# A weighted running average over 16 sequences: all v loads plain and rounded by VectorE, stores issued two slots later, the first state step moved

## The chip, the cores and the metric

The kernel runs on one core of a Trainium2 chip. The metric is the time of one execution on the device in microseconds (us). The median of four runs of the kernel before is 293.57 us (293.37 to 294.54).

The engines go by the names of the profile: PE is TensorE (matmul), PEld its weight loads, DVE is VectorE, ACT is ScalarE, POOL is GpSimd, and SP is SyncE, which here only issues DMAs. Each engine takes its instructions strictly in the order of the program; an instruction that waits holds up all behind it on that engine.

## The reference

For each of 16 batches and 256 channels a recurrence runs over 2048 time steps. Inputs are w and u (256 numbers each) and k and v (16 x 2048 x 256, float32, 33.55 MB each); the output has v's shape. Cut to what is computed:

```
for b, t:
    ww = u + k[b,t];  qq = max(pp, ww)
    e1 = exp(pp - qq);  e2 = exp(ww - qq)
    output[b,t] = (e1*aa + e2*v[b,t]) / (e1*bb + e2 + 1e-08)
    ww = pp - w + k[b,t];  qq = max(ww, k[b,t])
    e1 = exp(ww - qq);  e2 = exp(k[b,t] - qq)
    aa = e1*aa + e2*v[b,t];  bb = e1*bb + e2;  pp = qq
```

So every output is a quotient of two running sums, a numerator that carries v and a denominator without it, with a running maximum pp taken out of the exponents. Every input is read once (67.1 MB) and every output written once (33.5 MB).

## The kernel before, in words

**Tiles and slots.** Time is cut into 16 steps of 128 (NST), and the batches into 4 groups of 4. One tile n (64 of them, NP) is 128 time steps of 4 batches, 128 partitions by 1024 numbers, 512 KB of k and 512 KB of v. Tile n belongs to step c = n // 4. One turn of the main loop is a slot. Slots 0 to 9 (L427 to L447) only start tiles; from slot 10 on (L448 to L483), slot n starts tile n and also finishes the denominator of tile q = n - 10 (LAG is 10) and the numerator and output of tile qp = n - 11. After the last tile a closing loop (L487 to L510) finishes the remaining ones.

**What one tile needs.** `load_k` and `load_v` bring it in. `round_k` (L182, DVE) rounds k to float32r in `km`. `logs` (L191, L197, PE) makes exponents in PSUM out of k and of the decays. `exps` (L208 in the first ten slots, L210 later, ACT) turns them into weights in the ring EZR, which holds 12 tiles. `cast_v` (L223, DVE) rounds v to bf16 in `vb`. `times_v` (L228, DVE) multiplies the weights with vb, in EZR too. `sums` (L252, PE) adds up each half step for the state. Ten slots later `den` (L358, PE) makes the denominators, `recip` (L364 and L366, ACT: a logarithm and an exponential) their reciprocals in a buffer `rd`, `num` (L371, PE) the numerators, half a tile at a time in one PSUM bank NUMB, and `mult` (L375, DVE) the output, in place in rd. `store` (L378) sends rd out.

**Two kinds of v load.** `v_mode` says "dma" for n >= 10 with n % 4 == 3 (14 tiles): there GpSimd issues a DMA that converts float32 to bf16 on the way, straight into vb (L68), and `cast_v` does nothing. The other 50 v loads are plain loads by SyncE (L71), rounded by DVE.

**SyncE's queue.** At the head of slot n SyncE is given the loads six tiles ahead (AHEAD), for n + 6 < 16 as v of tile n + 5 and k of tile n + 6, later as k and v of tile n + 6; near the end of slot n the store of tile n - 11. The buffers are 6 for k, 5 for v, 4 for vb, 6 for rd; an issue waits until the buffer's last user is done. GpSimd issues the converting load of tile 4c + 11 in `state_next` of step c.

**The state.** Each step c needs one pass of small work that takes its sums to the ring: `copy_sums`, `turn`, `state_logs` (L274, ACT), `state_frames` (L283), `state_scan` (L287, DVE), `state_offsets` (L296 to L300), `state_weights` (L304, ACT), `state_chain` (L313 to L318, DVE), `turn_back` (L337, PE), `inject` (a cast on DVE, L343, and four DMAs of 8 KB by GpSimd into EZR, L348), `state_next` (L327, L328, GpSimd). Frames and offsets are on DVE for steps 0, 1 and 15, on GpSimd for the others. The list `plan` (L391 to L407) names for each of them a slot, counted from s = 4c + 3, and a place within the slot; `small_work(n, place)` issues what is due there. Step 0's state is first needed by the denominators of tile 0 to 3 in slots 10 to 13.

Of the kernel before, what the change touches and what calls it, by code (L numbers as in the profile page):

```python
# [7 lines left out]
F32 = mybir.dt.float32  # L8
F32R = mybir.dt.float32r
BF16 = mybir.dt.bfloat16  # L10
ALU = mybir.AluOpType
ACT = mybir.ActivationFunctionType
# [3 lines left out]
def kernel(  # L16
# [9 lines left out]
    K = tc.keep_in_program_order  # L26
    PE, DVE, SC, POOL, SP = nc.tensor, nc.vector, nc.scalar, nc.gpsimd, nc.sync

    B, T, Dm = k.shape
# [4 lines left out]
    NP = 4 * NST  # L34
    RING = 12
    AHEAD = 6
    LAG = 10
# [5 lines left out]
    kpool = ctx.enter_context(tc.tile_pool(name="kpool", bufs=AHEAD))  # L43
    vpool = ctx.enter_context(tc.tile_pool(name="vpool", bufs=5))
    vbpool = ctx.enter_context(tc.tile_pool(name="vbpool", bufs=4))
    rpool = ctx.enter_context(tc.tile_pool(name="rpool", bufs=6))
    small = ctx.enter_context(tc.tile_pool(name="small", bufs=2))
    tiny = ctx.enter_context(tc.tile_pool(name="tiny", bufs=1))
    ps = ctx.enter_context(tc.tile_pool(name="ps", bufs=1, space=bass.MemoryType.PSUM))


    kr_of, vr_of, VB = {}, {}, {}

    def v_mode(n):
        return "dma" if n >= LAG and n % 4 == 3 else "dve"

    def rows_of(x, n):
        c, p = divmod(n, 4)
        return x[4 * p:4 * p + 4, c * TC:(c + 1) * TC, :].rearrange("n t d -> t n d")

    def load_k(n, queue=SP):
        kr_of[n] = kpool.tile([128, 4, Dm], F32, tag="kr", name="kr")
        K(queue.dma_start(out=kr_of[n], in_=rows_of(k, n)))

    def load_v(n, queue=SP):
        if v_mode(n) == "dma":
            VB[n] = vbpool.tile([128, 4, Dm], BF16, tag="vb", name="vb")
            K(POOL.dma_start(out=VB[n], in_=rows_of(v, n)))  # L68
        else:
            vr_of[n] = vpool.tile([128, 4, Dm], F32, tag="vr", name="vr")  # L70
            K(queue.dma_start(out=vr_of[n], in_=rows_of(v, n)))  # L71


    def load(n):
        for x, f in ((n - 1, load_v), (n, load_k)) if n < LAG + AHEAD else ((n, load_k), (n, load_v)):
            if x < NP and (f == load_k or v_mode(x) != "dma"):
                f(x)

# [32 lines left out]
    load_k(1)  # L113
    load_row(SP, 1, 2, u)
    load_v(0)
    for n in range(2, AHEAD):
        load_k(n)
# [62 lines left out]
    def round_k(n):  # L180
        km = consts.tile([128, 4, Dm], F32R, tag=f"km{n % 2}", name="km") if n < 2 else KM[n - 2]
        K(DVE.tensor_copy(km, kr_of.pop(n)))  # L182
        KM[n] = km
# [21 lines left out]
    def exps(n):  # L205
        if n < TURNS:
            for q in range(2):
                K(SC.activation(ez(n)[:, q], half(n, q), ACT.Exp))  # L208
        else:
            K(SC.activation(ez(n)[:, 0:2], PS[:, 0:4, :].rearrange("p (q i) x -> p q i x", q=2), ACT.Exp))  # L210

    def cast_v(n):
        mode = v_mode(n)
        if mode == "dma":
            return
        vb = vbpool.tile([128, 4, Dm], BF16, tag="vb", name="vb")
        vr = vr_of.pop(n)
        if mode == "act":
            K(SC.activation(vb, vr, ACT.Copy))
        elif mode == "pool":  # L220
            K(POOL.tensor_copy(vb, vr))
        else:
            K(DVE.tensor_copy(vb, vr))  # L223
        VB[n] = vb

    def times_v(n):
        vb = VB.pop(n).rearrange("p (i n) d -> p i (n d)", i=2)
        K(DVE.tensor_mul(ez(n)[:, 2:4], ez(n)[:, 0:2], vb.unsqueeze(1).broadcast_to([128, 2, 2, D])))  # L228
# [94 lines left out]
    def state_next(c):  # L323
        G, tb = st.pop((c, "G")), st.pop((c, "tb"))
        AB, nxt = AB_of[c % 2], AB_of[(c + 1) % 2]
        y = tiny.tile([128, 2, 32], F32, tag="y", name="y")
        K(POOL.tensor_mul(y, AB[:, :, 1, :], G[:, 1, :].unsqueeze(1).broadcast_to([128, 2, 32])))  # L327
        K(POOL.tensor_add(nxt[:, :, 0, :], y, tb[:, :, 1, :]))  # L328

        if 4 * c + 11 < NP:  # L330
            load_v(4 * c + 11)


    def turn_back(c):
        t = MISC[:, Dm:Dm + 128]
# [19 lines left out]
    def den(n):  # L355
        for m, q in (("L", 0), ("Id", 1)):
            for i in range(2):
                K(PE.matmul(DENB[:, i, :], mats[m], ez(n)[:, q, i, :], start=q == 0, stop=q == 1,  # L358
                            skip_group_check=True))
# [9 lines left out]
    def num(n, bank, i):  # L369
        for m, q in (("LN", 2), ("IdN", 3)):  # L370
            K(PE.matmul(bank, mats[m], ez(n)[:, q, i, :], start=q == 2, stop=q == 3, skip_group_check=True))  # L371

    def mult(n, bank, i):
        rd = RD[n]
        K(DVE.tensor_mul(rd[:, i, :], bank, rd[:, i, :]))  # L375

    def store(n):
        K(SP.dma_start(out=rows_of(out, n), in_=RD.pop(n).rearrange("p i (n d) -> p (i n) d", n=2)))  # L378
# [10 lines left out]
    for c in range(NST):  # L389
        s = 4 * c + 3  # L390
        plan = [(s + 1, "act" if s + 1 < LAG else "recip", copy_sums), (s + 1, "pe", turn),  # L391
                (s + 2, "act", state_logs), (s + 2, "mid", state_frames), (s + 2, "scan", state_scan), (s + 2, "scan", state_offsets),
                (s + 3, "recip", state_weights), (s + 3, "chain", state_chain),
                (s + 4, "nums", turn_back), (s + 4, "mid", inject), (s + 4, "mid", state_next)]
        if c == 0:
            plan = [(s + 1, "act", copy_sums), (s + 1, "pe", turn), (s + 2, "act", state_logs),
                    (s + 2, "chain", state_frames), (s + 2, "chain", state_scan), (s + 2, "chain", state_offsets),
                    (s + 3, "act", state_weights), (s + 3, "chain", state_chain),
                    (s + 4, "logs", turn_back), (s + 4, "logs", inject), (s + 4, "round", state_next)]
        if c == 1:  # L400
            plan = [(s + 1, "act", copy_sums), (s + 1, "pe", turn), (s + 2, "act", state_logs),
                    (s + 2, "chain", state_frames), (s + 2, "chain", state_scan), (s + 2, "chain", state_offsets)] + plan[6:]
        if c == NST - 1:
            plan = [(s + 1, "copy", copy_sums), (s + 1, "turn", turn),
                    (s + 1, "post", state_logs), (s + 1, "mid", state_frames), (s + 1, "mid", state_scan), (s + 1, "mid", state_offsets),
                    (s + 2, "post", state_weights), (s + 2, "first", state_chain),
                    (s + 3, "turn", turn_back), (s + 3, "first", inject)]  # L407
        for slot, where, f in plan:
            later.setdefault((slot, where), []).append((f, c))

    def small_work(n, where):
        for f, c in later.pop((n, where), []):
            f(c)
# [10 lines left out]
    logs(0)  # L424
    round_k(1)
    cast_v(0)
    for n in range(LAG):  # L427

# [19 lines left out]
    for n in range(LAG, NP):  # L448

        q, qp = n - LAG, n - LAG - 1  # L450
        load(n + AHEAD)
        if qp >= 0:
            num(qp, NUMB, 0)
        den(q)
        small_work(n, "nums")
        exps(n)
        small_work(n, "act")
        if qp >= 0:
            mult(qp, NUMB, 0)
        small_work(n, "mid")  # L460
        if n + 2 < NP:
            round_k(n + 2)
        if n + 1 < NP:
            cast_v(n + 1)
        else:
            times_v(n)
        if qp >= 0:
            num(qp, NUMB, 1)

        sums(n - 1)  # L470
        recip(q, lambda: small_work(n, "recip"))
        if qp >= 0:
            mult(qp, NUMB, 1)
        small_work(n, "scan")
        if qp >= 0:
            store(qp)
        if n + 1 < NP:
            times_v(n)
            small_work(n, "chain")
            logs(n + 1)  # L480
        else:
            den(q + 1)
        small_work(n, "pe")  # L483
    sums(NP - 1)
    small_work(NP, "copy")
    late = []
    for n in range(NP, NP + LAG + 1):  # L487

        q, qp = n - LAG, n - LAG - 1
        H = PS[:, 2 * (n % 2):2 * (n % 2) + 2, :]  # L490
        for i in range(2):
            num(qp, H[:, i, :], i)
        small_work(n, "turn")
        if q < NP:
            recip(q, lambda: small_work(n, "recip"))
        small_work(n, "post")
        if q + 1 < NP:
            den(q + 1)
        small_work(n, "first")
        if qp == NP - 1:  # L500
            last_outputs(qp, H)
            break
        late.append((qp, H))
        if n != NP + 1:

            for x, bank in late:
                mult(x, bank, slice(0, 2))
                store(x)
            late = []
        small_work(n, "mid")  # L510
# [31 lines left out]
```

## Time and profile before

| what | value |
|---|---|
| median of the runs | 293.57 us (293.37 to 294.54, 4 runs) |
| the profiled execution's own time | 294.03 us |
| its span, first to last instruction | 292.3 us |
| busy: PE, DVE, ACT, POOL | 262.7, 256.2, 257.0, 119.4 us |
| granted clock of TensorE | 0.996 of full speed |
| HBM read and written | 67.12 MB and 33.55 MB, 344 GB/s over the span |
| SyncE's queue; GpSimd's queue | 93.08 MB; 4.20 MB |
| k load, v load, store, converting load: issue to landing | 9.1, 9.1, 8.6, 8.7 us |
| DVE: one L375, L182, L223, L228 | 732, 716, 720, 1216 ns |
| ACT: one L210, L364, L366 | 1875, 1013, 1046 ns |
| DVE waiting for a k tile | 12.9 us, 28 times |

A profile comes from one execution. Busy time is that in which an engine has an instruction in work; issuing DMAs and waiting are not counted. A row of groups reads: line, engine, operation, what it writes and reads, how often, then busy time and the mean of one in ns, then how long the engine stood idle just before them and what it was waiting for. The slices are 40 equal parts of the span (7.3 us each), with the busy share in tenths. GB/s counts a transfer by the bytes that it writes, so a converting load counts half of what it reads.

### The profile page before, as it was taken

Reading aid. Unit: us, or ns where it says so; the run is one execution under the profiler, and the core shown is the slowest. Engines: PE = TensorE matmul, PEld = TensorE weight load, DVE = VectorE, ACT = ScalarE, POOL = GpSimd, SP = SyncE. Lnnn points to the kernel's source line nnn. Section 1 sums busy time; section 2 is a strip of 40 time slices with the busy share of each in tenths; the row PEclk is TensorE's granted clock in tenths of the full one; section 3 lists DMA queues with packets and bytes.
Section 4 is the critical chain, followed back from the end, with each engine's and each line's share of the span. In section 5 each row is a group of like instructions: output and inputs, shape, how many; then the busy total and the mean of one; then the engine's idle time right before and its main releaser. Section 6 shows DMA issues by size and latency. Waiting matters only on the chain. (4 is left out here: it accounts for less than half of the span.)

```text
span 292.3 us, 4969 instructions
## 1 busy us (share of the span) xinstructions
PE 262.7 (90%) x1694; PEld 119.8 (41%) x1694; DVE 256.2 (88%) x439; ACT 257.0 (88%) x253; POOL 119.4 (41%) x226
## 2 busy tenths in 40 slices
PE   6997898999999999998898999998899989988881
PEld 1443433445444444443443444444344444433330
DVE  4699999999999999998989999897998989886753
ACT  2586788999999999999899999989899998999892
POOL 7000425453535445554534455551455545242200
PEclk9999999999999999999999999999999999999998
DMA  6999999999999999999999999999999999974686
GB/s 222 349 348 348 348 306 347 300 386 315 382 340 372 362 350 381 333 379 332 379 344 372 375 336 383 330 380 330 376 372 337 380 335 383 329 276 152 217 290 215
DMA packets 103522, 97.86 MB, mean 335 GB/s; under 512 B 4157, under 2 KB 103497, under 8 KB 103497
## 3 DMA queue, kind: packets, MB, share of 16 engines
q1 hardware_dynamic: 93752, 93.08, 94.5%
q0 software_dynamic: 9440, 4.20, 10.0%
q8 instruction: 13, 0.21, 0.3%
q10 hardware_dynamic: 304, 0.27, 0.3%
q14 instruction: 13, 0.10, 0.1%
HBM read 67.12 MB, written 33.55 MB: 344 GB/s over the span
## 5 line engine op out<-in xcount | busy, mean ns | idle before, releaser
L210 ACT ACTIVATE EZR<-PS 128x2048 bf16<-128x2048 f32 x54 | 101.3, 1875 | 6.3 <-PE PS L197 5.4
L375 DVE TENSOR_TENSOR rd<-PS,rd 128x512 f32<-128x512 f32 (+1 forms) x118 | 86.1, 732 | 7.7 <-PE PS L371 6.6
L228 DVE TENSOR_TENSOR EZR<-EZR,vb 128x2048 bf16<-128x2048 bf16 x64 | 77.8, 1216 | 3.5 <-ACT EZR L208 2.6
L366 ACT ACTIVATE rd<-rd 128x1024 f32<-128x1024 f32 (+1 forms) x65 | 68.0, 1046 | 1.2
L364 ACT ACTIVATE rd<-PS 128x1024 f32<-128x1024 f32 (+1 forms) x65 | 65.9, 1013 | 2.0 <-PE PS L358 1.8
L348 POOL DMA_DIRECT2D EZR<-cb x64 | 38.5, 607 | 61.4 <-DVE cb L343 49.6
L371 PE MATMUL PS<-EZR,LN 128*128 128x512 bf16 x128 | 48.6, 380 | 11.9 <-DVE rd L375 8.1
L182 DVE CAST km<-kr 128x1024 fp32r<-128x1024 f32 x64 | 45.8, 716 | 13.1 <-DMA kr<-in_k_dram 12.9
L197 PE MATMUL PS<-km,NLE 128*128 128x512 f32 x128 | 47.6, 454 | 2.3 <-DVE km L182 2.0
L371 PE MATMUL PS<-EZR,IdN 128*128 128x512 bf16 x128 | 48.4, 378 | 0.0
L197 PE MATMUL PS<-km,NLZ 128*128 128x512 f32 x128 | 41.0, 402 | 0.0
L358 PE MATMUL PS<-EZR,L 128*128 128x512 bf16 x128 | 38.0, 379 | 1.8 <-ACT rd L364 1.7
L358 PE MATMUL PS<-EZR,Id 128*128 128x512 bf16 x128 | 38.1, 379 | 0.0
L223 DVE CAST vb<-vr 128x1024 bf16<-128x1024 f32 x50 | 36.0, 720 | 0.0
L191 PE MATMUL PS<-WU,CO 32*128 32x512 bf16 x256 | 26.4, 391 | 2.3 <-DVE WU L423 1.9
L283 POOL TENSOR_TENSOR F<-LL,LL 128x32 f32<-128x32 f32 x13 | 7.6, 583 | 51.0 <-ACT LL L274 51.0
L208 ACT ACTIVATE EZR<-PS 128x1024 bf16<-128x1024 f32 x20 | 19.4, 1021 | 8.7 <-PE PS L197 8.7
L197 PEld LDWEIGHTS PS<-km,NLZ 128*128 128x128 f32 x128 | 24.6, 192 | 5.8
L197 PEld LDWEIGHTS PS<-km,NLE 128*128 128x128 f32 x128 | 19.4, 191 | 17.5 <-issue 12.7
L252 PE MATMUL PS<-EZR,OH 128*32 128x256 bf16 x512 | 25.8, 278 | 0.1
L371 PEld LDWEIGHTS <-IdN 128*128 128x128 bf16 x128 | 12.4, 97 | 27.7 <-issue 24.9
L296 POOL TENSOR_TENSOR Q<-P,F 128x64 f32<-128x64 f32 x13 | 15.6, 1203 | 13.0 <-DVE P L287 13.0
(72 smaller groups left out, 212.5 us busy)
## 6 DMA issues: line engine op xcount, KB each, us to landing
kr<-in_k_dram SPq DMA_DIRECT2D x64, 512.0 KB, 9.1
out_dram<-rd SPq DMA_DIRECT2D x63, 512.0 KB, 8.6
vr<-in_v_dram SPq DMA_DIRECT2D x50, 512.0 KB, 9.1
vb<-in_v_dram POOLq DMA_DIRECT2D x14, 256.0 KB, 8.7
EZR<-cb POOLq DMA_DIRECT2D x64, 8.0 KB, 5.3
out_dram<-rd SPq DMA_DIRECT2D x2, 128.0 KB, 3.0
out_dram<-rd ACTq DMA_DIRECT2D x2, 128.0 KB, 3.2
wuf<-in_w_dram ACTq DMA_DIRECT2D x1, 8.0 KB
```

The lines of the kernel that those rows point to most:

```text
L182: K(DVE.tensor_copy(km, kr_of.pop(n)))
L191: K(PE.matmul(half(n, q)[:, i, :], CO[g:g + 32, :], WU[g:g + 32, :].unsqueeze(1).broadcast_to([32, 2, Dm]), start=True, stop=False, tile_p ...
L197: K(PE.matmul(half(n, q)[:, i, :], (NLE, NLZ)[q], km[:, i, :], start=False, stop=True, skip_group_check=True))
L210: K(SC.activation(ez(n)[:, 0:2], PS[:, 0:4, :].rearrange("p (q i) x -> p q i x", q=2), ACT.Exp))
L223: K(DVE.tensor_copy(vb, vr))
L228: K(DVE.tensor_mul(ez(n)[:, 2:4], ez(n)[:, 0:2], vb.unsqueeze(1).broadcast_to([128, 2, 2, D])))
L348: K(POOL.dma_start(out=EZR[r:r + 1, 2 * q, r0:r0 + 4, :, :].rearrange("o p i (b x) -> o (p i b) x", b=4), in_=cb[x:x + 32, :]))
L358: K(PE.matmul(DENB[:, i, :], mats[m], ez(n)[:, q, i, :], start=q == 0, stop=q == 1, skip_group_check=True))
L364: K(SC.activation(rd[:, i, :], DENB[:, i, :], ACT.Ln, scale=RS))
L366: K(SC.activation(rd[:, i, :], rd[:, i, :], ACT.Exp, scale=-1.0))
L371: K(PE.matmul(bank, mats[m], ez(n)[:, q, i, :], start=q == 2, stop=q == 3, skip_group_check=True))
L375: K(DVE.tensor_mul(rd[:, i, :], bank, rd[:, i, :]))
```

## The change

It has four parts.

- `v_mode` and the converting loads go. All 64 v loads are plain ones by SyncE, in the order v of tile n + 5, k of tile n + 6 at the head of slot n, and DVE rounds all 64. In the main loop the rounding of a tile with n % 4 == 3 stands in its own slot n, right ahead of that of tile n + 1; in slots with n % 4 == 2 there is none.
- The store of tile n - 13 (before: n - 11) is issued at the head of slot n, right behind the two loads (before: near the slot's end). Two stores are made up ahead of the closing loop. rd has 8 buffers (before: 6).
- The small work of step 0: `state_logs`, frames, scan and offsets are due in slot 4 (before: 5), `state_weights` and `state_chain` in slot 5 (6), `turn_back`, `inject` and `state_next` in slot 6 (7). What was done on DVE ahead of `round_k` ("chain") comes behind it ("round").
- For step 1 frames, scan and offsets stay in slot 9 and also move from "chain" to "round".

```diff
-    rpool = ctx.enter_context(tc.tile_pool(name="rpool", bufs=6))
+    rpool = ctx.enter_context(tc.tile_pool(name="rpool", bufs=8))
...
-    def v_mode(n):
-        return "dma" if n >= LAG and n % 4 == 3 else "dve"
...
     def load_v(n, queue=SP):
-        if v_mode(n) == "dma":
-            VB[n] = vbpool.tile([128, 4, Dm], BF16, tag="vb", name="vb")
-            K(POOL.dma_start(out=VB[n], in_=rows_of(v, n)))
-        else:
-            vr_of[n] = vpool.tile([128, 4, Dm], F32, tag="vr", name="vr")
-            K(queue.dma_start(out=vr_of[n], in_=rows_of(v, n)))
+        vr_of[n] = vpool.tile([128, 4, Dm], F32, tag="vr", name="vr")
+        K(queue.dma_start(out=vr_of[n], in_=rows_of(v, n)))
...
     def load(n):
-        for x, f in ((n - 1, load_v), (n, load_k)) if n < LAG + AHEAD else ((n, load_k), (n, load_v)):
-            if x < NP and (f == load_k or v_mode(x) != "dma"):
-                f(x)
+        if n - 1 < NP:
+            load_v(n - 1)
+        if n < NP:
+            load_k(n)
...
-        if 4 * c + 11 < NP:
-            load_v(4 * c + 11)
...
         if c == 0:
-            plan = [(s + 1, "act", copy_sums), (s + 1, "pe", turn), (s + 2, "act", state_logs),
-                    (s + 2, "chain", state_frames), (s + 2, "chain", state_scan), (s + 2, "chain", state_offsets),
-                    (s + 3, "act", state_weights), (s + 3, "chain", state_chain),
-                    (s + 4, "logs", turn_back), (s + 4, "logs", inject), (s + 4, "round", state_next)]
+            plan = [(s + 1, "act", copy_sums), (s + 1, "pe", turn), (s + 1, "pe", state_logs),
+                    (s + 1, "round", state_frames), (s + 1, "round", state_scan), (s + 1, "round", state_offsets),
+                    (s + 2, "act", state_weights), (s + 2, "round", state_chain),
+                    (s + 3, "pe", turn_back), (s + 3, "round", inject), (s + 3, "round", state_next)]
         if c == 1:
             plan = [(s + 1, "act", copy_sums), (s + 1, "pe", turn), (s + 2, "act", state_logs),
-                    (s + 2, "chain", state_frames), (s + 2, "chain", state_scan), (s + 2, "chain", state_offsets)] + plan[6:]
+                    (s + 2, "round", state_frames), (s + 2, "round", state_scan), (s + 2, "round", state_offsets)] + plan[6:]
...
         load(n + AHEAD)
+
+        if qp >= 2:
+            store(qp - 2)
...
             round_k(n + 2)
+
+        if n % 4 == 3:
+            cast_v(n)
         if n + 1 < NP:
-            cast_v(n + 1)
+            if n % 4 != 2:
+                cast_v(n + 1)
...
-        if qp >= 0:
-            store(qp)
...
     late = []
+    store(NP - LAG - 3)
+    store(NP - LAG - 2)
```

More of the change, by code (lines that the diff above doesn't have):

```diff
@@ L212, in cast_v @@
     def cast_v(n):
-        mode = v_mode(n)
-        if mode == "dma":
-            return
         vb = vbpool.tile([128, 4, Dm], BF16, tag="vb", name="vb")
         vr = vr_of.pop(n)
[L218 to L223, printed above, removed]
+        K(DVE.tensor_copy(vb, vr))
         VB[n] = vb
```

## The prediction

> **What bounds the kernel now.** I read the 40 slices first, then the cycle of four slots (one step of the state each) in two stages, then who waits, then the transfer rate, and the end.
>
> ```profile
> PE   6997898999999999998898999998899989988881
> ...
> DVE  4699999999999999998989999897998989886753
> ACT  2586788999999999999899999989899998999892
> ...
> DMA  6999999999999999999999999999999999974686
> ```
>
> From slice 2 to slice 35 nothing is idle, the DMA engines least of all. So averages don't tell; the length of four slots does (start of one L210 to the fourth after it):
>
> ```profile
> 79.71:95.53 15.82, 15.56 (x105) 7.24 (x104) 15.42 (x26) 15.65 (x15) 7.83 (x15) 1.00 1.12 358
> 95.53:111.34 15.81, 15.55 (x105) 7.23 (x104) 15.42 (x26) 15.66 (x16) 7.80 (x15) 1.00 1.12 358
> ...
> 162.40:179.18 16.78, 15.69 (x105) 7.21 (x104) 15.47 (x26) 15.77 (x15) 8.13 (x15) 1.00 1.12 359
> 179.18:196.06 16.88, 15.69 (x105) 7.22 (x104) 15.47 (x26) 15.78 (x15) 8.24 (x15) 1.00 1.12 359
> ```
>
> Columns: stretch, length, busy PE, PEld, DVE, ACT, POOL, clock, DMA share, GB/s. Up to slot 30 (119.30 us) four slots take 15.81, with ACT 15.66 busy and DVE 15.42: they are bound by computing. Later they take 16.8 to 17.6 (127.88 to 247.29 is 119.41 for 28 slots, 17.06 per four) with the same busy times. What fills the difference:
>
> ```profile
> L182 DVE CAST km<-kr 128x1024 fp32r<-128x1024 f32 x28 | 20.7, 739 | 10.3 <-DMA kr<-in_k_dram 10.3
> ```
>
> That is the group of 127.9 to 247.3. DVE waits 10.3 us for k tiles; from 64 to 112 the same group waits 0.0. So computing, late after the start, catches up with the loads by slot 31, and from there the transfers set the pace: the last k lands at 253.4 (the rounding there waited 0.62 for it), slot 63 starts at 259.91, and the end follows at a fixed distance in a chain of L358 and L364 (2.13 us per pair of batches).
>
> **The transfers.** SyncE's queue is paced by the transfers: the k load that the code has in slot 29 goes out at 125.81, when computing is in slot 31. The order in that queue is what counts, not the moment at which a store's data is ready.
>
> ```profile
> 14.00:24.00 10.00, 9.79 (x80) 4.63 (x76) 9.91 (x23) 7.92 (x10) 0.00 (x0) 1.00 1.09 348
> ```
>
> ```profile
> 120.00:130.00 10.00, 9.09 (x65) 3.77 (x63) 9.18 (x17) 9.26 (x9) 6.17 (x12) 1.00 1.09 377
> ...
> 140.00:151.00 11.00, 9.98 (x65) 4.67 (x64) 9.95 (x17) 10.24 (x9) 4.65 (x7) 1.00 1.09 378
> ...
> 156.00:168.00 12.00, 11.46 (x80) 5.49 (x80) 11.43 (x19) 11.04 (x11) 4.86 (x9) 1.00 1.09 379
> ```
>
> Loads alone run at 348 GB/s: 0.524 MB in 1.51 us. Loads and stores without a converting load run at 378 (small state writes included): 1.387 us. A converting load counts only its 0.262 MB written; from 133 to 137, where one runs, the rate reads 287 to 291.
>
> **The change, part by part.**
>
> *Converting load to plain load.* Four slots move 11 transfers by SyncE (15.26 us at 1.387) and one converting load. The five cycles nearest each other after 127.88 (16.98, 16.78, 16.88, 16.80, 16.83) average 16.85, so the converting load costs 1.6; the plain one costs 1.39. Gain 0.2 for each of the 13 ahead of the last k: 2.6 us. Bounds: with 17.06 per four, 1.80 and a gain of 5.4; from the other side, if the clean rate holds only while a second queue runs in turn with SyncE's, 12 x 1.51 = 18.1 per four, a loss of 1.0 x 12.25. I take 2.6, since the 377 to 379 rows hold almost nothing but SyncE's transfers. GpSimd also loses 14 issues (12.6 us busy), and they slow a cast beside them (0.89 against 0.69 at 97.38): 0.2 per four slots back to DVE.
>
> The Trainium skill, "DMA: Bandwidth & Descriptors", section Specifications, gives HBM about 358 GB/s per core. By that 6.29 MB per four slots would take 17.57, the kernel some 6 us slower before the stores' gain. The rows of 377 to 379 go past it, so the sum doesn't use it.
>
> *Stores two slots behind.* In slot 57 the last k load had 46 stores ahead of it in the queue; now it has 44. Two transfers of 1.387: 2.8 us sooner. Against it, loads run alone for some four transfers more at 1.51: +0.5. At the end the DMA engines have room (digits 4 to 8), and the two stores made up ahead of the last slots cost nothing. The eight buffers: a store leaves SyncE at slot q+13, about two slots behind computing, lands 8.9 us (two slots) later, about q+17, and its buffer is wanted at q+18. One slot of cover; gone, the Ln of L364 waits for a store and ACT with it.
>
> *The added wait.* For n%4==3 the v load at the head of slot n (tile n+5, five buffers) waits for the rounding in mid slot n; queued behind it are a k load and a store. SyncE is two slots late already, and 9.1 us from issue to landing is some six transfers queued, so 2 us of wait are covered: nothing. Without that cover up to 2 us a time in the early stage, where computing leads.
>
> *DVE.* 14 casts of 686 ns, 0.60 from start to start (126.19 to 126.79): 15.42 + 0.60 to 0.69, less 0.2 of contention, is 15.8 to 16.1 per four slots against ACT's 15.81. So the floor is 15.8 to 16.1, but slot n%4==3 now has both casts ahead of its second multiply:
>
> ```profile
> 95.05 1.22 DVE L228 TENSOR_TENSOR EZR<-EZR,vb 128x2048 bf16<-128x2048 bf16 x1
> ...
> 96.18 0.68 DVE L375 TENSOR_TENSOR rd<-PS,rd 128x512 f32<-128x512 f32 x1
> ...
> 96.92 0.38 PE L371 MATMUL PS<-EZR,LN 128*128 128x512 bf16 x1
> ```
>
> The first multiply of slot 24 starts as DVE finishes times_v, PE's second numerator as the multiply ends, and logs and the next L210 stand behind it with 0.1 to 0.2 us to spare. A cast more ahead of it makes ACT wait up to 0.45 in one slot of four: 16.25 at worst by these rows, 15.8 at best. I take 16.25: the 0.1 to 0.2 is measured, while the contention that would give time back is seen only at single casts. The Trainium skill, "SBUF — State Buffer", section Who interferes with whom, adds that a cast that uses both VectorE ports keeps GpSimd out entirely; no wait here is priced by it, and the sum leaves it out (the trace has ACT waiting 4.5 us for GpSimd's offsets between 125 and 250, so it would be seen there).
>
> *First steps.* For c=0 all its work moves about one slot sooner: two ACT instructions (0.36 each), on DVE frames, scan and offsets (1.3), chain (0.9), cast (0.29), PE's turn back, GpSimd's offsets and next, and its four 8 KB writes (issued at 33.08, 2.4 us). Behind the roundings instead of ahead, it frees logs of slots 6 to 8, where ACT waited 0.98 and 1.55. What is late next is k10: DVE waited 0.39 for it at 36.63, with loads at 348, so nothing is left by slot 10. Then v11 stands in SyncE's queue ahead of k12, which lands four loads after k10, 36.63 + 4 x 1.51 = 42.7, while its rounding started at 41.98 (0.7), and slot 11 has one cast more (0.6). For c=1, 1.3 us of DVE pass behind a rounding; ACT was continuous there. Together +0.6: the bounds are -1.3 (the passed rounding) and +1.3 (0.7 + 0.6), and I take half the upper one, since k12's wait can hide in DVE's queue.
>
> **The sum.** Transfers: -2.6 - 2.8 + 0.5 = -4.9. Computing: slots 14 to 63 took 259.91 - 55.93 = 203.98; 12.25 x 16.25 = 199.1, with the start -4.9 + 0.6 = -4.3. The later one ends: -4.3. The profiled execution took 294.03 (span 292.3): 289.7. The median of the runs, 293.57, is 0.46 lower: **289.3**.
>
> **Rivals.**
> - *Nothing couples* (0.15): 15.9 per four slots and the transfers' 5.4 for the converting loads. -5.4 - 2.8 + 0.5 = -7.7 for transfers, -9.2 + 0.6 for computing: 285.9. For it: DVE 15.42 busy has room. Against: PE's small margin.
> - *DVE and PE become the bound* (0.15): the double cast costs its full 0.6 and the start its 1.3, 16.45 per four slots: 201.5, -2.5 + 1.3 = -1.2 in all: 292.4. Same, if 16.5 or more.
> - *SyncE alone is slower* (0.18): a single queue with no second one beside it keeps to 355 GB/s, nearer the 348 row: 12 x 1.477 = 17.7 per four, 0.65 more x 12.25 = +8.0, stores -2.3: 299.3. It decides against me from about 369 GB/s down (6.29 MB in 17.06). For it: 348 wherever no GpSimd transfer and no store runs. Against: 377 to 379.
> - *The order buys nothing* (0.07): stores go out when the ring has room either way, and the last k comes no sooner: only the 2.6 of the transfers, less the start's 1.3: -1.3, 292.3.
>
> My forecast has 0.45: 287.5 to 291. Measurement tells 0.3%, 0.9 us, from no change: faster is under 292.7. Faster: the forecast (0.45), the first rival (0.15), half of the second (0.08) and of the fourth (0.04): 0.72. Same: their other halves, 0.10. Slower: the third, 0.18. The range reaches from the first rival to 294.4, where only the slower case is left out with half of the first.
>
> **What would show it.** L223 64 times, L68 gone, GpSimd busy near 107. Cycles of 16.0 to 16.4 in both stages; DVE's wait for kr under 6 us (now 12.9); clean rate still about 378 all through, no dips; last k landing near 248.7; the same chain at the end. Wrong if the rate reads under 369, if L364 waits for a store, or if cycles before slot 30 go over 16.6 with ACT waiting for PE.

## The result and the profile after

The changed kernel takes 293.21 us in the median (292.17 to 295.25, 43 runs), the kernel before 293.83 on the same chips (293.13 to 294.87, 64 runs). The ratio is 0.9981, 95% interval 0.9974 to 0.9987: faster by 0.2%, some 0.6 us, where 4.3 us were forecast. That is below the 0.9 us from which the prediction would call a change a change, an outcome to which it gave 0.10, and the time lies outside the 287.5 to 291 of its forecast. The profiled execution took 294.14 us (span 292.4), 0.9 above its median; that is kept in mind below.

Lines of code have moved. L210 is now L204, L375 is L358, L182 is L176, L223 is L209, L228 is L214, L197 is L191, L371 is L354, L337 is L320, L364 is L347.

From the page of the changed kernel, the slices:

```profile
PE   6996896999999999999999999999999999998881
...
DVE  4798989899999999999999999999999999986853
ACT  2675675999999999999999999999999999999892
...
PEclk9799997999999999999999999999999999999998
DMA  7999999999999999999999999999999999964686
```

The dips of PE, DVE and ACT in the later half are gone, yet the end is where it was. ACT is lower in slices 3 to 7 (7, 5, 6, 7, 5 where it had 8, 6, 7, 8, 8), and PE's clock has a 7 in slice 7. So something was gained in the steady part and lost at the start. The cycles of four slots say how much (columns as before: stretch, length, busy PE, PEld, DVE, ACT, POOL, clock, DMA share, GB/s):

```profile
75.39:91.81 16.42, 15.64 (x105) 7.22 (x104) 15.83 (x27) 15.95 (x15) 7.57 (x14) 1.00 1.09 376
173.91:190.32 16.41, 15.62 (x105) 7.22 (x104) 15.82 (x27) 15.95 (x16) 7.58 (x14) 1.00 1.09 379
```

Two stages have become one. Where the kernel before had 15.8 and then 16.8, the cycles are 16.41 and 16.42. And VectorE no longer waits for tiles after the start (from 60 to 260 us it has no wait for a load). From the page, the two groups of roundings, k and v:

```profile
L176 DVE CAST km<-kr 128x1024 fp32r<-128x1024 f32 x64 | 43.8, 685 | 2.5 <-DMA kr<-in_k_dram 2.4
L209 DVE CAST vb<-vr 128x1024 bf16<-128x1024 f32 x64 | 43.3, 694 | 2.4 <-DMA vr<-in_v_dram 2.2
```

The account by slots: slot 14 starts at 59.05 instead of 55.93, 3.1 us later. From there to slot 63 it is 200.84 instead of 203.98, 3.1 us less. Slot 63 starts at 259.89 instead of 259.91, and the closing part is the same chain as before. In this profile the two cancel to the last digit, which is chance.

### The profile page after: what moved, and what is told of

Read it like the earlier page. It is cut to its first block, busy times and chain, and to the rows that moved or that the text cites. A ratio compares the mean times of both kernels' runs of the same rounds, so it can differ in the third digit from the quotient of the medians.

```text
span 292.4 us, 5013 instructions
## 1 busy us (share of the span) xinstructions
PE 263.8 (90%) x1694; PEld 120.2 (41%) x1694; DVE 261.9 (90%) x453; ACT 258.6 (88%) x253; POOL 114.0 (39%) x212
## 5 line engine op out<-in xcount | busy, mean ns | idle before, releaser
L204 ACT ACTIVATE EZR<-PS 128x2048 bf16<-128x2048 f32 x54 | 101.1, 1873 | 7.0 <-PE PS L191 4.4
L358 DVE TENSOR_TENSOR rd<-PS,rd 128x512 f32<-128x512 f32 (+1 forms) x118 | 86.6, 736 | 13.7 <-PE PS L354 7.9
L214 DVE TENSOR_TENSOR EZR<-EZR,vb 128x2048 bf16<-128x2048 bf16 x64 | 78.5, 1227 | 0.8 <-ACT EZR L202 0.2
L347 ACT ACTIVATE rd<-PS 128x1024 f32<-128x1024 f32 (+1 forms) x65 | 65.6, 1010 | 1.4 <-PE PS L341 1.3
L331 POOL DMA_DIRECT2D EZR<-cb x64 | 40.1, 631 | 60.6 <-DVE cb L326 47.4
L354 PE MATMUL PS<-EZR,LN 128*128 128x512 bf16 x128 | 48.8, 382 | 10.3 <-DVE rd L358 7.5
L191 PE MATMUL PS<-km,NLE 128*128 128x512 f32 x128 | 47.7, 454 | 2.9 <-DVE km L176 2.9
L354 PE MATMUL PS<-EZR,IdN 128*128 128x512 bf16 x128 | 48.6, 380 | 0.0
L176 DVE CAST km<-kr 128x1024 fp32r<-128x1024 f32 x64 | 43.8, 685 | 2.5 <-DMA kr<-in_k_dram 2.4
L209 DVE CAST vb<-vr 128x1024 bf16<-128x1024 f32 x64 | 43.3, 694 | 2.4 <-DMA vr<-in_v_dram 2.2
L191 PE MATMUL PS<-km,NLZ 128*128 128x512 f32 x128 | 40.8, 400 | 0.0
L269 POOL TENSOR_TENSOR F<-LL,LL 128x32 f32<-128x32 f32 x13 | 9.5, 728 | 62.1 <-ACT LL L260 62.1
L185 PE MATMUL PS<-WU,CO 32*128 32x512 bf16 x256 | 27.2, 391 | 3.0 <-DVE WU L406 1.6
L191 PEld LDWEIGHTS PS<-km,NLZ 128*128 128x128 f32 x128 | 24.6, 192 | 5.8
L191 PEld LDWEIGHTS PS<-km,NLE 128*128 128x128 f32 x128 | 19.4, 191 | 18.1 <-issue 12.5
L354 PEld LDWEIGHTS <-IdN 128*128 128x128 bf16 x128 | 12.4, 97 | 26.1 <-issue 23.7
L354 PEld LDWEIGHTS <-LN 128*128 128x128 bf16 x128 | 12.8, 100 | 18.3 <-issue 11.3
```

The lines of the kernel that those rows point to most:

```text
L185: K(PE.matmul(half(n, q)[:, i, :], CO[g:g + 32, :], WU[g:g + 32, :].unsqueeze(1).broadcast_to([32, 2, Dm]), start=True, stop=False, tile_p ...
L191: K(PE.matmul(half(n, q)[:, i, :], (NLE, NLZ)[q], km[:, i, :], start=False, stop=True, skip_group_check=True))
L331: K(POOL.dma_start(out=EZR[r:r + 1, 2 * q, r0:r0 + 4, :, :].rearrange("o p i (b x) -> o (p i b) x", b=4), in_=cb[x:x + 32, :]))
L347: K(SC.activation(rd[:, i, :], DENB[:, i, :], ACT.Ln, scale=RS))
```

## The experiments

A summary first. Time ratios are to the kernel before on the same chip; slot starts and cycles are of one profile each. Early is the mean of four slots from slot 18 to 30, late from slot 42 to 62.

| run | median us | ratio, 95% interval | slot 14 | slot 63 | four slots, early / late |
|---|---|---|---|---|---|
| before | 293.83 | | 55.93 | 259.91 | 15.81 / 16.98 |
| before again | | | 56.05 | 259.53 | 15.89 / 16.91 |
| changed | 293.21 | 0.9981 (0.9974 to 0.9987) | 59.05 | 259.89 | 16.42 / 16.42 |
| old plan | 292.85 | 0.9974 (0.9961 to 0.9987) | 57.94 | 258.88 | 16.42 / 16.42 |
| casts spread | 292.91 | 0.9971 (0.9955 to 0.9986) | 58.06 | 258.73 | 15.88 / 16.89 |
| no third cast | 291.93 | 0.9931 (0.9915 to 0.9947) | 56.88 | 257.75 | 15.82 / 17.07 |
| half the stores | 292.03 | 0.9946 (0.9931 to 0.9962) | 58.02 | 258.94 | 16.43 / 16.42 |
| plan only | 293.78 | 1.0002 (0.9993 to 1.0011) | 56.81 | 259.91 | 15.81 / 16.98 |
| stores only | 291.83 | 0.9938 (0.9919 to 0.9957) | 56.74 | 257.92 | 15.83 / 16.97 |
| plain loads only | 293.25 | 0.9986 (0.9973 to 1.0000) | 56.91 | 258.72 | 16.43 / 16.54 |
| step 1 old | 292.99 | 0.9974 (0.9961 to 0.9987) | 56.96 | 257.98 | 16.42 / 16.43 |
| stores three behind, 8 buffers | 292.73 | 0.9956 (0.9943 to 0.9970) | 56.18 | 258.30 | 15.82 / 16.94 |
| spread, three behind, 9 buffers | 291.52 | 0.9914 (0.9899 to 0.9929) | 57.16 | 257.27 | 15.98 / 16.80 |

### What sets 16.41 us per four slots

6.29 MB in 16.41 us is 383 GB/s, about the best that the transfers showed in any slice of before (up to 386; the rows above read 376 and 379). So the first question was whether the cycle is the transfers' or VectorE's. Three edits to the changed kernel tell it. The first stores two of the four batches of each tile, so that half of the output of every tile but the last is missing:

```diff
-        K(SP.dma_start(out=rows_of(out, n), in_=RD.pop(n).rearrange("p i (n d) -> p (i n) d", n=2)))
+        K(SP.dma_start(out=rows_of(out, n)[:, 0:2, :], in_=RD.pop(n)[:, 0, :].rearrange("p (n d) -> p n d", n=2)))
```

> Stores only two of the four batches of each tile in the main part, so half of the output is not written and four slots move 5.24 MB instead of 6.29. Theory V: the cycle stays at 16.4 and the time within 1 us of the changed kernel. Rival D: the cycle falls toward 15.9, the time by 5 us or more.

Measured: a sixth of the bytes is gone, and the cycle does not move. The run with half the stores, same columns:

```profile
74.36:90.77 16.41, 15.62 (x105) 7.22 (x104) 15.82 (x27) 15.96 (x15) 7.57 (x14) 1.00 1.01 326
172.93:189.34 16.41, 15.62 (x105) 7.21 (x104) 15.82 (x27) 15.95 (x17) 7.57 (x14) 1.00 1.02 325
```

The rate falls to 326 GB/s and nothing else changes: the transfers follow, they don't lead. (Its time is 1.2 us below the changed kernel's, 1.0 by the ratios, at the edge of the "within 1 us" that was expected. In its profile slot 63 starts 0.95 us earlier, which it already had at slot 10, and from there to the end it is 0.85 shorter, since the closing part too stores half: neither is the cycle's.)

The second keeps all 64 casts and deals them out otherwise:

```diff
-        if n % 4 == 3:
-            cast_v(n)
-        if n + 1 < NP:
-            if n % 4 != 2:
-                cast_v(n + 1)
-        else:
+        if n % 4 == 0 and n >= LAG + 2:
+            cast_v(n + 1)
+            cast_v(n + 2)
+        elif n % 4 == 1 and n >= LAG + 2:
+            cast_v(n + 2)
...
+        elif n % 4 == 3 and n + 1 < NP:
+            cast_v(n + 1)
+        if n + 1 == NP:
             times_v(n)
```

> The changed kernel with the same casts dealt out otherwise from slot 12 on: two in slots n%4==0, one in n%4==1 and n%4==3, none in n%4==2, each at least as early as before. Theory V (the cycle of 16.41 us per four slots is set by VectorE's order in slots n%4==3, not by transfers): the cycle falls to 15.85 to 16.1 as long as loads lead, the time by 3 to 5 us, or until VectorE waits for k tiles. Rival D (16.41 is the transfers' own pace, 6.29 MB at 383 GB/s): cycle stays at 16.4, VectorE shows waits for k or v tiles, time unchanged.

```profile
73.89:89.77 15.88, 15.53 (x105) 7.17 (x104) 15.73 (x27) 15.70 (x16) 6.97 (x14) 1.00 1.09 375
216.27:233.10 16.83, 15.66 (x106) 7.21 (x106) 15.94 (x27) 15.77 (x16) 6.54 (x13) 1.00 1.09 379
```

Same instructions, same 27 on DVE per cycle, 0.53 us less. DVE is busy 15.73 of 15.88 there: it does have room for 64 casts, and it was their place that cost. But only up to slot 38. Then the lead of the loads is used up (VectorE waits for v tiles, 5.1 us in 8 waits after 140), and the cycle is 16.83 again, like that of before. So both theories had a part: VectorE's order set the changed kernel's cycle, and just behind it stand the transfers. The 3 to 5 us expected did not come.

The third leaves out the cast of the tiles with n % 4 == 3, which multiply a tile of zeros instead of v; the loads stay:

```diff
         if n % 4 == 3:
-            cast_v(n)
+            vr_of.pop(n)
+            VB[n] = FIX
```

> Leaves out the casts of tiles n%4==3 from slot 11 on (13 casts and that of tile 11): those tiles multiply a fixed tile of zeros instead of v; the loads stay. Theory V: the cycle falls to 15.8 to 15.9, ScalarE's own pace, until the transfers limit, and the time by 4 us or more. Rival D: the cycle stays at 16.4, time within 1 us of the changed kernel.

The early cycle is 15.82, as in the kernel before (15.81), so a cast in that place cost 0.6 us in each cycle, all of its 0.60. From slot 42 on the transfers take over, at 17.07 (VectorE waits 9.1 us for k tiles after 140). Slot 63 starts 2.1 us sooner than in the changed kernel, but so does slot 14; from there to slot 63 the two take 200.87 and 200.84. The time falls by 1.3, not by the 4 expected.

The path can be read in the changed kernel itself, slots 39 and 40, VectorE's timeline (start, length, then the instruction):

```profile
163.16 0.69 DVE L176 CAST km<-kr 128x1024 fp32r<-128x1024 f32 x1
163.76 1.29 DVE L209 CAST vb<-vr 128x1024 bf16<-128x1024 f32 x2
164.96 0.68 DVE L358 TENSOR_TENSOR rd<-PS,rd 128x512 f32<-128x512 f32 x1
165.56 1.22 DVE L214 TENSOR_TENSOR EZR<-EZR,vb 128x2048 bf16<-128x2048 bf16 x1
166.69 0.68 DVE L358 TENSOR_TENSOR rd<-PS,rd 128x512 f32<-128x512 f32 x1
```

and PE's, beside it:

```profile
165.70 0.38 PE L354 MATMUL PS<-EZR,LN 128*128 128x512 bf16 x1 [0.30 <-DVE rd L358]
...
167.43 0.38 PE L354 MATMUL PS<-EZR,LN 128*128 128x512 bf16 x1 [0.28 <-DVE rd L358]
...
168.61 0.73 PE L191 MATMUL PS<-km,NLE 128*128 128x512 f32 x2
169.18 0.62 PE L191 MATMUL PS<-km,NLZ 128*128 128x512 f32 x2
```

Both casts (1.29) stand ahead of slot 39's second multiply (164.96), and PE's first numerator of slot 40 waits 0.30 for it. So times_v and the first multiply of slot 40 are a cast later too, and PE's second numerator waits 0.28 for that. Behind these in PE's order stand sums and logs, which ScalarE needs: slot 40 takes 4.40 us instead of 3.89. In the cycle from 75.39 to 91.81 PE has the same two waits, 0.29 and 0.28, and no other; in the cycle of before from 79.71, and in the early cycles with the casts spread or one left out, it waits for nothing. Together, 0.57, they match the 0.53 to 0.60 that a cycle lost. VectorE itself then stands idle 0.44 a cycle until PE's numerator ends (5.8 us ahead of L358 between 60 and 250, 4.4 of it booked as "issue"), which is why its busy share never shows it as the limit.

### Each part alone

Stores two slots later with eight buffers, all else as before:

```diff
         load(n + AHEAD)
+        if qp >= 2:
+            store(qp - 2)
...
-        if qp >= 0:
-            store(qp)
```

> The kernel before with the stores two slots later and eight buffers, nothing else. Theory Q (the order in SyncE's queue sets when the last k lands): two transfers fewer ahead of it, the later cycles stay at 16.8 but begin later, slot 63 starts 2 to 3 us sooner than 259.91, time 290.7 to 291.7. Rival (the order buys nothing): 293.4 to 294.

```profile
72.67:88.51 15.84, 15.23 (x103) 7.23 (x104) 15.45 (x26) 15.66 (x17) 7.84 (x15) 1.00 1.11 355
181.37:198.14 16.77, 15.33 (x104) 7.21 (x106) 15.45 (x26) 15.78 (x16) 8.13 (x14) 1.00 1.11 360
```

The cycles are those of before, early and late; the late ones begin at slot 38 instead of 30, and slot 63 starts 2.0 us sooner. The order in the queue does buy time, 1.8 us by the ratio, a little less than the 2.3 of the sum (2.8 less 0.5); 291.83 is 0.1 above what was expected. No logarithm waits for a store with these eight buffers. This part alone beats the whole change.

Plain loads alone, with stores and first steps as before:

```diff
-        return "dma" if n >= LAG and n % 4 == 3 else "dve"
+        return "dve"
```

(the loads in the order and the casts in the places of the changed kernel).

> The kernel before with plain v loads and the 14 casts placed as in the changed kernel, stores and first steps as before. Theory V with the transfers' pace as the spread casts showed it: cycles of 16.4 from slot 14 on, then 16.8 once the loads are late, so little changes at the end: 293.5 to 295.5. The prediction's own term (a plain load is 0.2 us cheaper than a converting one for the transfers): slot 63 some 2.6 us sooner, 291 or below.

It is 293.25, just under the 293.5 to 295.5 expected. Its cycles are 16.4 up to slot 56, and from there 16.98, as the transfers catch up. It has the loads and stores of before ahead of its last k, only that 13 of them no longer convert: that k lands at 252.29, where two profiles of before have 253.42 and 253.13, so 0.8 to 1.1 us sooner, and not the 2.6 of the sum. The price of a plain load against a converting one is told by a comparison with the same order of stores. With all loads plain and the transfers in the lead, the late cycles are 16.89 (casts spread) and 17.07 (no third cast); with 14 loads converting they are 16.97 (stores only), 16.98 and 16.91 (before, twice). Slot 63 starts at 257.75 with no third cast and at 257.92 with the stores only. So for the transfers the two kinds cost the same to within 0.1 us a load, as far as these runs tell.

The moved first steps alone:

```diff
+            plan = [(s + 1, "act", copy_sums), (s + 1, "pe", turn), (s + 1, "pe", state_logs),
...
+                    (s + 2, "round", state_frames), (s + 2, "round", state_scan), (s + 2, "round", state_offsets)] + plan[6:]
```

> The kernel before with the moved small work of steps 0 and 1 and nothing else. Theory K (step 1's frames, put behind the rounding of k11, now wait for that tile to land; its chain comes a microsecond later, PE stands still over 2 us at turn_back in slot 11 and its clock is halved after it): slot 14 starts 1 to 3 us later than 55.93; the end, which the transfers set, moves less: 293.5 to 295. Rival S (the late start comes from v11 in SyncE's queue and its cast): slot 14 within 0.5 us of before, no halved clock near slot 11, time within 0.5 us.

Nothing, 1.0002. Slot 14 is at 56.81, PE waits 1.85 at turn_back in slot 11 (0.90 before) and keeps its full clock there. Expected were 1 to 3 us of delay at slot 14, a stop of over 2 us and a halved clock after it; the delay is 0.8 to 0.9, against two profiles of before, and neither of the others came.

### The start

> The kernel before once more, for a second profile of its start. If the halved clock of PE between 8 and 16 us and a slot 14 at 56.7 to 57 come with the execution and not with the change, they show here too; if they belong to the change, slot 14 is at 55.9 again with a full clock.

The kernel before once more: slot 14 at 56.05, the same within 0.12 us, though this execution has a 5 for PE's clock in its second slice and the first one had none. So that early dip comes with the execution, and by slot 14 it cost 0.12. Stores alone, which has the same code as before up to slot 11, has slot 14 at 56.74: 0.8 us is the scatter of the start.

The changed kernel's 59.05 is beyond that; with half the stores, the same code up to slot 13, it is 58.02. It helps to split the start at slot 10:

| run | first steps | v11 | slot 10 | slot 10 to slot 14 |
|---|---|---|---|---|
| before; again | old | converting | 38.83; 39.45 | 17.10; 16.60 |
| plan only | moved | converting | 39.28 | 17.53 |
| plain loads only | old | plain | 39.97 | 16.94 |
| old plan | old | plain | 41.04 | 16.90 |
| step 1 old | step 0 moved | plain | 38.94 | 18.02 |
| no third cast | moved | plain, no cast | 38.88 | 18.00 |
| changed | moved | plain | 39.60 | 19.45 |
| half the stores | moved | plain | 38.59 | 19.43 |
| casts spread | moved | plain | 38.60 | 19.46 |

Slot 10 comes early or late by a microsecond with the same code. But from slot 10 to 14 the three profiles that have both the moved steps and v11's cast agree to 0.03 us, 2.3 to 2.9 above before, and neither the steps alone (17.53) nor the plain loads alone (16.94) do that. The changed kernel's profile shows where: VectorE waits for k11 with everything behind it (slot 9), then for k12 (slot 10).

```profile
40.84 0.70 DVE L176 CAST km<-kr 128x1024 fp32r<-128x1024 f32 x1 [0.70 <-DMA kr<-in_k_dram]
41.45 0.20 DVE L269 TENSOR_TENSOR F<-LL,LL 128x32 f32<-128x32 f32 x1
...
43.75 0.69 DVE L176 CAST km<-kr 128x1024 fp32r<-128x1024 f32 x1 [0.25 <-DMA kr<-in_k_dram]
44.36 1.22 DVE L214 TENSOR_TENSOR EZR<-EZR,vb 128x2048 bf16<-128x2048 bf16 x1
45.49 0.22 DVE L299 TENSOR_TENSOR x<-AB,G 128x64 f32<-128x64 f32 x1
...
46.20 0.44 DVE L304 TENSOR_TENSOR CB<-AB,G 128x128 bf16<-128x128 f32 x1
```

Before, step 1's frames stood ahead of the rounding of k11 and filled the time until it landed:

```profile
39.41 0.20 DVE L283 TENSOR_TENSOR F<-LL,LL 128x32 f32<-128x32 f32 x1
...
40.72 0.75 DVE L182 CAST km<-kr 128x1024 fp32r<-128x1024 f32 x1
...
44.43 0.44 DVE L318 TENSOR_TENSOR CB<-AB,G 128x128 bf16<-128x128 f32 x1
```

Behind it they wait too. CB, the matrix that turn_back multiplies, comes at 46.64 instead of 44.87, and PE, with turn_back next in its order, stands still (PE's timeline of the changed kernel):

```profile
46.70 0.40 PE L320 MATMUL PS<-Id,CB 128*128 128x128 bf16 x4 [2.31 <-DVE CB L304]
...
49.25 1.22 PE L191 MATMUL PS<-km,NLE 128*128 128x512 f32 x2
```

and a stretch of its windows:

```profile
48.00:50.00 2.00, 2.00 (x15) 0.90 (x15) 2.00 (x5) 0.07 (x1) 2.00 (x4) 0.50 1.09 348
```

After 2.31 us of standing still PE runs at 0.50 of its clock (the column before the last two), and the two matmuls of L191 take 1.22 instead of 0.73; ACT is busy 0.07 of 2.00. Slot 12 starts 6.89 us after slot 11, 4.96 before. To test it, both steps or step 1 alone go back to their places in the changed kernel:

```diff
-                    (s + 2, "round", state_frames), (s + 2, "round", state_scan), (s + 2, "round", state_offsets)] + plan[6:]
+                    (s + 2, "chain", state_frames), (s + 2, "chain", state_scan), (s + 2, "chain", state_offsets)] + plan[6:]
```

> The changed kernel with step 1's frames, scan and offsets back ahead of the rounding in slot 9, step 0 left moved. Theory K: VectorE no longer waits for k11 ahead of the frames, PE's wait at turn_back in slot 11 falls from 2.3 to about 1.3 us, no halved clock there, slot 12 starts near 48.5 and slot 14 near 56.7 instead of 58 to 59; with the cycle at 16.4 the time falls to 291.5 to 292. Rival S: no change in slots 11 and 12, time within 0.4 us of the changed kernel.

> The changed kernel with the small work of steps 0 and 1 where it was before. Theory P (the moved first steps cost the start): the loss of 3.1 us up to slot 14 goes for the most part, slot 14 starts near 56.5 instead of 59.05, the time falls to about 290.5 to 291.5. Rival S (the start is late because v11 stands in SyncE's queue and loads run alone for longer): slot 14 stays near 59, the time within 0.5 us of the changed kernel. The cycle of four slots stays 16.4 in both.

With step 1 back, PE waits 1.66, keeps its clock, and slot 14 starts at 56.96, 1.1 to 2.1 sooner, as expected of that theory. With both back slot 14 is at 57.94, where rival S had "near 59" and the theory 56.5, and that too can be read. From slot 10 on it takes 16.90, so nothing of the loss is left although v11 stands in SyncE's queue as before, which speaks against rival S. What is late is slot 10, at 41.04: with step 0's frames ahead of a rounding again, PE stands still at an earlier place, and here its clock is halved after it (PE's timeline, and a stretch of windows, both of the old plan):

```profile
29.61 1.22 PE L191 MATMUL PS<-km,NLE 128*128 128x512 f32 x2 [1.86 <-DVE km L176]
...
30.00:32.00 2.00, 2.00 (x12) 0.90 (x11) 1.38 (x2) 1.13 (x2) 0.00 (x0) 0.50 1.09 347
```

All seven profiles with the old first steps have this stop, of 1.83 to 1.86 us, none with the moved ones has one of over 1.4 there, and the clock fell after it in two (old plan, plain loads only). So moving step 0 did remove a stop, as the prediction had it, while step 1's move lengthened another (0.90 before, 1.66 with step 1 back, 2.31).

And the times hardly follow: 292.99 and 292.85 against 293.21, intervals that overlap, where 291.5 to 292 and 290.5 to 291.5 were expected. So the wait, the halved clock and their cause are shown in the profiles, one of each kernel; that the order of the first steps makes more than half a microsecond in the median is not. The profiled execution of the changed kernel stands 0.9 us above its median, and its start may be part of that.

The Trainium skill, "TensorE: Matmul & The Clock Gate", section Why this matters for your kernels, asks for no gaps over about 3 us between bursts of matmuls. Here the clock was halved after 2.31 in the changed kernel, after 2.37 in two others (spread casts, half the stores), and after 1.86 and 1.85 in the old plan and the plain loads only; it was not after 2.33 in the run with no third cast, nor after 1.83 to 1.85 in five others with the old first steps. So stops well under 3 us did cost the clock in these rows, and the length of the stop alone doesn't tell whether.

### Stores later still

Stores three slots later, in the kernel before with eight buffers:

```diff
+        if qp >= 3:
+            store(qp - 3)
```

> The kernel before with the stores three slots later instead of two, still eight buffers (the 9th doesn't fit beside the converting loads). Theory Q: one transfer fewer ahead of the last k, slot 63 about 1 us sooner than with two (257.9), time 290.8 to 291.2. Rival (the buffers run out): ScalarE's logarithm waits for stores in the later cycles, time equal to that of two slots (291.8) or above.

The rival holds. From the waits of that run (who waited for whom: total, times, longest):

```profile
ACT rd L364 <- DMA out_dram<-rd: 7.2, 21, 1.1
```

The logarithm waits 21 times for a store to leave its buffer, and 292.73 is behind the 291.83 of two slots (their intervals just overlap). This is the one slot of cover that the prediction named, gone. With plain loads there is room for a ninth buffer (vb needs three):

> The changed kernel with the first steps as before, the casts dealt out as in the spread run, stores three slots later with nine buffers (three for vb). Theory: 15.9 per four slots from slot 14 (near 57) until the transfers catch up near slot 45, then 16.84; slot 63 near 257, time 290.5 to 291.5. Rival (plain loads cost the transfers more than converting ones): it ends with or behind the changed kernel, 292.5 to 293.5.

291.52, ratio 0.9914, at the upper edge of the range expected, and the best ratio of the study; it is the changed kernel with the first steps as before, the casts spread, and stores three behind. Its time and that of the stores alone are 0.3 us apart on different chips, with intervals that overlap, so between those two the order is not settled.

## Why the prediction was wrong

The main forecast, 289.3, missed by 3.9 us. Point by point:

- **What bounds the kernel before** held: transfers from slot 31 on, computing ahead of it. So did the rate: the two cycles of the changed kernel above read 376 and 379 GB/s, over the 369 that was the point of decision. The rival "SyncE alone is slower" fell.
- **The step that failed first is the start**, "Together +0.6", of bounds -1.3 to +1.3. It was +3.1 in the profile and +2.1 in the run with the same code up to slot 13; in both 2.3 to 2.4 of it came between slots 10 and 14. What was missed is that work put behind a rounding waits for that rounding's tile: the prediction counted k12's late landing (0.7), but for step 1 it let the frames "pass behind a rounding" at no price, and saw neither that k11 lands only after the time at which its rounding now comes (0.70 of wait), nor that PE has turn_back next in its order and stands still for 2.31 us, with half its clock after it.
- **The cycle**, "16.25 at worst by these rows", was 16.40 from slot 14 to 63, 200.84 instead of 199.1: +1.7. The mechanism was the one described, at the place described; the size was off. The prediction let the delay be absorbed by PE's spare 0.1 to 0.2; spread and left-out casts show 0.53 to 0.6 of the cast's 0.60 to be lost, and the rows have it as two waits of PE, 0.29 and 0.28, where the prediction counted one of up to 0.45. The second rival, 16.45, was nearer in the cycle, and its 292.4 nearer in time.
- With the two sizes as measured, computing gives 200.84 - 203.98 + 3.1 = 0.0 in the profile and, with the start of 58.02, about -1.1; the ratio of the medians says -0.6.
- **The converting loads**, "Gain 0.2 for each", 2.6 us in all, gain 1.1 at most: by that much the last k came sooner with plain loads only, and the late cycles are 16.89 and 17.07 with plain loads, 16.91 to 16.98 with converting ones. The 1.387 us of a plain load came from stretches picked for having no dips; over whole late cycles 12 plain transfers take 1.41 to 1.42 each, small state writes and all, and 16.9 to 17.0 less 11 of these leaves about 1.4 for the converting one. It did not decide, as computing came last, but it would have: with spread casts the transfers end at 258.73, 1.2 us sooner than before, not 4.9 (they want two of four v tiles a slot earlier, too).
- **The stores**, "2.8 us sooner" less 0.5, held: 2.0 at slot 63, 1.8 in time. The cover of the buffers held as well: two slots with eight, and not three.
- **The added wait** for v's buffers showed no cost that could be told: VectorE waits for v 2.2 us in all, at the start.
- **What would show it**: 64 casts and no L68, held; cycles of 16.0 to 16.4, at the upper end; the wait for k under 6 us, 2.4; "the last k near 248.7": the last rounding of k is at 253.46 as before, and not for want of its tile; GpSimd "near 107" was 114.0. None of the three signs of being wrong appeared (a rate under 369, L364 waiting for a store, cycles over 16.6): none of them watched the start.

## What to carry to other kernels

Where one engine's order ties three others together, a spare tenth of busy time says nothing about where an added instruction can go: count what stands behind it on every engine until the loop closes, and if the loop has no slack, price it in full, as the 0.60 us of the cast were here. Work that moves behind a wait inherits the wait, so of a step that is moved ask what the instruction ahead of it is waiting for at its new moment. Where transfers set the pace, the order of a queue is worth about a transfer's time for each one moved behind (here 2.0 us for two stores), and it can be had alone.

## What was not expected of the hardware

- Converting on the way or not, a 512 KB load took about 1.4 us of the transfers' time, to within 0.1, though in the rows of a converting load the rate by bytes written fell from 378 to about 290.
- Loads alone stayed at 348 GB/s in the start of every run (14 to 24 us), and plain loads with stores went at 372 to 380 in the cycles that transfers set (spread casts, no third cast).
- PE's clock went to half after standing still 2.31 to 2.37 us in three profiles and 1.85 to 1.86 in two, and stayed full after 2.33 in one and 1.83 to 1.85 in six.
